# Reordering the opening of a conformer encoder step: tanh and the first modulation sums first, squares in one operation, the second modulation's sums between the first turns

## The chip, the cores and the metric

The kernel runs on one core of one Trainium2 chip. The metric is the device time of one execution in microseconds (us); the time before is the median of three runs. A core has five engines that run side by side and meet at semaphores: TensorE (PE, with its weight loads as PEld), VectorE (DVE), ScalarE (ACT), GpSimd (POOL) and SyncE (SP). Transfers are issued by SP and by ACT here; "SPq" and "ACTq" in the profile are those issues. Each engine takes its own instructions in the order in which the compiler has put them.

## The reference

One layer of a streaming encoder on 2048 prompt frames and 64 sample frames, D_MODEL = 1024, all in float32:

```python
mod = silu(c) @ w_ada + b_ada                 # 6 vectors of 1024 per batch
sh1, sc1, gt1, sh2, sc2, gt2 = split(mod, 6)
h = rms_norm(x, norm1_g) * (1 + sc1) + sh1
z = h @ w_in                                  # conv GLU pair | q | k | v | two gates
...                                           # conv branch, band attention, merge, output projection
x = x + gt1 * (merged @ w_o)
h2 = rms_norm(x, norm2_g) * (1 + sc2) + sh2
x = x + gt2 * ((silu(gate) * up) @ w_ffn_out) # gate, up = split(h2 @ w_ffn_in)
```

What matters here is the start: nothing of `z` can be multiplied before some of `sc1` and `sh1` (the product of silu(c) with `w_ada`) and the row norms of `x` are known.

## The kernel before

Float32 products are made from three products of a high and a low part (`mm3`): a weight `wst` is split into `whi` (a copy on ACT) and `wlo` (a subtraction on DVE or POOL), an activation `h` into `hh` and `hl` likewise. `Weights` (the object `W`) loads raw weights into at most three staging tiles `wst`, splits them in `split` and keeps up to `held` = 5 split ones; `W.reach` is how many `fill` may have split ahead, and `W.open("wst")` opens the second and third staging tile. `Slabs` (the object `M`) does the same for `w_ada`, in four buffers `wmod` of 512 KB; `M.get` and `M.done` use and free one, and a freed buffer is filled with the next slab.

The program is written in Python and unrolled. The compiler places the instructions on each engine: among those that it holds ready at a moment it takes the one written earliest, so an instruction written late can be placed early when its engine has a free moment. `with tc.issue_after(ins)` keeps every instruction of the block that runs on `ins`'s engine behind `ins`. The later blocks are interleaved by a planner in the program (`Stream`, `Lane`), which counts a load for each engine from assumed durations and lets side work step when these counts allow.

`first_block` computes the q columns of the first 576 rows, five row tiles `xs` (tile 0 is the sample's 64 rows, tiles 1 to 4 have 128 prompt rows), so that its parts can start as their inputs land:

- `setup` turns `c` into columns (`cc`), takes the tanh (`th`, ACT) for silu, and writes `cl` (DVE). `begun` holds the tanh and the write of `cl`. `vectors` transposes the loaded bias and norm vectors into `cols`.
- `modulation(ct)` multiplies `cl` with four slabs (`mod_sums`, into the PSUM tile `pa`: shift with two slabs, scale with two), copies the sums to `R` (`mod_rows`, DVE), and returns `rest`, which turns them into columns (`mod_columns`: four small products with `sel`, then DVE writes into `B1`, then again for `A1`). One call serves two of the eight 128-wide slices of D, `ct` and `ct + 1`.
- `scale_rows` takes the row norms: `square` (ACT, in two halves with a sum each, then a DVE add), `rsqrt_mean` (a small DVE operation `t`, a power on POOL `r`), and the scaling of the row tile on DVE.
- `turn(k)` transposes slice `k` of the five scaled row tiles into `pt` (PE), applies `A1` and `B1` (`h`, DVE), and splits it into `hh` (ACT) and `hl` (DVE).
- `product(i, k)` is the three matmuls of row tile `i` and slice `k` into `ps`. The loop over `k` runs `turn(k + 1)`, at even `k` the next `modulation(k + 2)`, and the five products. `product` needs split weight number `k // 2`.
- `first_rows` issues the loads of the five row tiles, `taps` (at `k == 2`) issues seven small loads on ACT, and `bias_rows`, written much later, loads the distance biases `rv` from ACT.

The order around the change before: the squares and scalings of tiles 0 and 1 are written ahead of `modulation(0)`, then `vectors`, `rest`, tiles 2 to 4, and `W.fill` (all behind `begun`); then `turn(0)`. In the loop, `modulation(2)` and `W.open("wst")` come at `k == 0` after the products of row tiles 0 and 1.

Of the kernel before, what the change touches and what calls it, by code (L numbers as in the profile page):

```python
# [8 lines left out]
F32 = mybir.dt.float32  # L9
F32R = mybir.dt.float32r  # L10
AF = mybir.ActivationFunctionType
# [5 lines left out]
P = 128  # L17
D = 1024
# [211 lines left out]
class Slabs:  # L230
# [8 lines left out]
    def fill(self):  # L239
        while len(self.ready) < min(len(self.keys), self.freed + self.held):  # L240
            (src,), a, b = self.source(self.keys[len(self.ready)])
            w = self.pool.tile([P, a, b], F32, tag="wmod", name="wmod", bufs=self.held)
            i = len(self.ready)
            (self.other if i < self.held and i % 2 else self.sync).dma_start(w, src)
            self.ready.append(w)

    def get(self, key):
# [364 lines left out]
def streaming_layer(ctx: ExitStack, tc: tile.TileContext, I, O):  # L612
    nc = tc.nc
# [121 lines left out]
    def rsqrt_mean(pool, ssq, n, width, count, bufs=5):  # L735
        t = pool.tile([P, 8], F32, tag="rs_t", bufs=bufs)
        r = pool.tile([P, 8], F32, tag="rs_r", bufs=bufs)
        dve.tensor_scalar(t[:n, :width], ssq, 1.0 / count, EPS, ALU.mult, ALU.add)
        stream.after("pool", "dve")
        gps.tensor_tensor(r[:n, :width], t[:n, :width], mhalf[:n, :width], ALU.pow)  # L740
        return r[:n, :width]
# [117 lines left out]
    def mod_rows(pa):  # L859
        R = temp("R", pa.shape)  # L860
        stream.after("dve", "pe")
        dve.tensor_copy(R, pa)
        return R

# [41 lines left out]

    def first_rows():
        places = ((wa, "x", 3), (wa, "x", 3), (wa, "x", 3), (wk, "kk", 1), (wk, "q2", 1))
        queues = (nc.sync, nc.sync, nc.scalar, nc.sync, nc.scalar)
        return [load_x(*tl, *place, q) for tl, place, q in zip(token_tiles(*PBLOCKS[0]), places, queues)]  # L910

    def first_block(xs):

        tiles = token_tiles(*PBLOCKS[0])
        vectors, taps, begun = setup()
        taps = taps()

        def scale_rows(a, b):
            for x_t, (t, n) in list(zip(xs, tiles))[a:b]:
                r = square(x_t, n)  # L920
                dve.tensor_scalar(x_t[:n], x_t[:n], r, None, ALU.mult)

        def modulation(ct):

            pa = ps_a.tile([P, 512], F32, tag="o", name="pa")
            cs = [slice(c6 * 2 * P, (c6 + 1) * 2 * P) for c6 in range(2)]

            with tc.issue_after(pe.last.ins):
                for c6, c in enumerate(cs):
                    mod_sums(pa[:, c], [("mod", c6, ct // 2, h, 0) for h in range(2)])  # L930
            R = mod_rows(pa)

            def rest():
                for c6, c in enumerate(cs):
                    mod_columns(pa[:, c], R[:, c], c6, ct, 1)

            return rest

        def turn(k):
            pt = ps_a.tile([P, 2, 512], F32, tag="s", name="pt")  # L940
            for i, (t, n) in enumerate(tiles):
                o = pt[:, 0, t : t + n] if i < 4 else pt[:, 1, :n]
                pe.transpose(o, xs[i][:n, k * P : (k + 1) * P], ident[:n, :n])
            h = wk.tile([P, QB + SMP], F32, tag="pr", name="h32", bufs=8)
            for a, e, o, w in ((0, SMP, pt[:, 0, :SMP], 1), (SMP, 448, pt[:, 0, SMP:448], 0), (448, 576, pt[:, 1, :P], 0)):
                dve.tensor_scalar(h[:, a:e], o, A1[:, k, w : w + 1], B1[:, k, w : w + 1], ALU.mult, ALU.add)

            for c in (slice(0, 448), slice(448, 576)) if not k else (slice(0, 576),):
                split(hh[:, k, c], hl[:, k, c], h[:, c])


        with tc.issue_after(begun[0]), tc.issue_after(begun[1]):
            scale_rows(0, 2)
            rest = modulation(0)
            vectors()
            rest()
            sums_turned = pe.last.ins
            with tc.issue_after(dve.last.ins):
                scale_rows(2, 5)
            with tc.issue_after(act.last.ins), tc.issue_after(dve.last.ins):  # L960
                W.reach = W.held
                W.fill()
        with tc.issue_after(sums_turned):
            turn(0)
        pss = [ps_g.tile([P, 512], F32, tag="gp", name="ps") for _ in tiles]
        ws = {}

        def product(i, k):
            t, n = tiles[i]
            if k // 2 not in ws:  # L970
                ws[k // 2] = W.get(("qkv", 0, k // 2))
            wh, wl = ws[k // 2]
            mm3(pss[i][:n], hh[:, k, t : t + n], hl[:, k, t : t + n], wh[:, k % 2], wl[:, k % 2], k == 0, k == KT - 1)
            if i == len(tiles) - 1 and k % 2:
                W.done()

        for k in range(KT - 2):
            if k == 2:
                with tc.issue_after(act.last.ins):
                    next(taps)  # L980
            turn(k + 1)
            if k and k % 2 == 0:
                rest = modulation(k + 2)
            for i in range(len(tiles)):
                if i == 2 and not k:
                    rest = modulation(k + 2)
                    W.open("wst")
                if i == (2 if k else 4) and k % 2 == 0:
                    rest()
                product(i, k)  # L990
        turn(KT - 1)
        for i, (t, n) in enumerate(tiles):
            for k in (KT - 2, KT - 1):
                product(i, k)
            work.start(qk_rows(pss[i], n, gqk[:, 0:1], q_d, t, None, i > 2))
        next(taps, None)

    bias = wk.tile([P, 640], F32, name="bias")

    def bias_rows():  # L1000
        rv = wk.tile([NH, 257], F32, tag="vv", name="rv", bufs=2)
        nc.scalar.dma_start(rv, I["rel_bias"].rearrange("l h r -> (l h) r"))
        rr = wk.tile([NH, 768], F32, tag="kk", name="rr", bufs=1)

        dve.tensor_scalar(rr[:, :256], rv[:, 1:], 8.0, None, ALU.mult)
        dve.memset(rr[:, 256:], 0.0)
        dve.tensor_scalar(rr[:, 256:], rr[:, 256:], rv[:, 256:], 8.0, ALU.add, ALU.mult)
        nc.scalar.dma_start(rb_d, rr)

        for r, c in ((0, 0), (HD, 576)):  # L1010
            dve.memset(bias[r : r + HD, c : c + HD], BIG)
# [122 lines left out]
        queue.dma_start(x_t[:n], rows(x_p, x_s, t, n))  # L1134
        return x_t

    def square(x_t, n):
        ssq = wk.tile([P, 2], F32, tag="ssq", name="ssq", bufs=3)
        for j in range(2):
            act.activation(temp("junk")[:n], x_t[:n, 512 * j : 512 * j + 512], AF.Square, accum_out=ssq[:n, j : j + 1])  # L1140
        stream.after("dve", "act")
        dve.tensor_tensor(ssq[:n, 0:1], ssq[:n, 0:1], ssq[:n, 1:2], ALU.add)
        return rsqrt_mean(wk, ssq[:n, 0:1], n, 1, D)
# [76 lines left out]
    YW = UW - HIST  # L1220
# [602 lines left out]
    for s, (lo, hi) in enumerate(CBLOCKS):  # L1823
# [195 lines left out]
        def rest(f, z, y):  # L2019


            if not seven(s, f):
                hidden(f, 1, y)
                return
            if "t" not in sums:
                sums["t"] = wk.tile([P, 4, 2, CW // 2], F32R, tag="m1", name="sums")
            at = lambda i: [sums["t"][:, i, l, :half] for l in range(2)]
            if f % 2 == 0:
                sums["a21"], sums["s3"] = (
                    wk.tile([P, CW // 2], F32, tag=name, name=name, bufs=1)[:, :half] for name in ("a21", "s3")  # L2030
                )
                stream.after("act", "dve")
                act.activation(sums["a21"], y, AF.Copy)
                stream.after("dve", "act")
                dve.tensor_tensor(y, z, sums["a21"], ALU.subtract)
                stream.after("act", "dve")
                split(*at(2), y)
                act.activation(sums["s3"], y, AF.Copy)
                return
            hidden(f, 1, y)  # L2040
            t = bank("gp")
            dve.tensor_tensor(t, y, sums["a21"], ALU.add)
            dve.tensor_tensor(y, y, sums["s3"], ALU.subtract)
# [253 lines left out]
```

## Time and profile before

| | |
|---|---|
| time, median of 3 runs (lowest to highest) | 2979.57 us (2976.84 to 2982.91) |
| the profiled execution's own time | 2979.5 us |
| its span, first to last instruction | 2977.7 us |
| TensorE busy | 2900.2 us (97% of the span) |
| VectorE busy | 2025.9 us (68%) |
| ScalarE busy | 1356.8 us (46%) |
| GpSimd busy | 1127.7 us (38%) |
| first matmul of the q product | starts 28.26 us into the span |
| mean granted TensorE clock | 0.995 |

The times in the profile count from the first instruction. A row of the timeline has the start, the duration, the engine (or its queue of issues), the line, the operation, what it writes and reads, shapes and a count, and in brackets how long the engine stood idle before it and what ended that. All engine calls pass through one helper, so nearly all rows carry its line, L102; tiles are told apart by their names. A row of the windows has the busy time of each engine in one stretch, the granted clock of TensorE, the busy share of the 16 DMA engines (which can come out slightly over 1) and the rate of transfers.

### The profile page before, as it was taken

How to read it: one execution, taken by the hardware profiler on the slowest of the kernel's cores; microseconds unless marked ns; L12 is line 12 of the kernel's file. 1: busy time of each engine (PE TensorE's matmuls, PEld its weight loads, DVE VectorE, ACT ScalarE, POOL GpSimd, SP SyncE). 2: the span in 40 equal slices, each digit the busy share in tenths (PEclk: the TensorE clock that was granted, in tenths of full speed). 3: DMA queues.
4: the chain of work that ended last, by engine and by line, in shares of the span. 5: the costliest groups of instructions: out<-in, count | busy, mean ns of one | idle time of the engine just before them, and what ended most of it. 6: DMA issues, size and time to landing. Idle time of an engine off the chain costs nothing.

```text
span 2977.7 us, 44838 instructions
## 1 busy us (share of the span) xinstructions
PE 2900.2 (97%) x16199; PEld 2593.1 (87%) x16199; DVE 2025.9 (68%) x3637; ACT 1356.8 (46%) x2441; POOL 1127.7 (38%) x727
## 2 busy tenths in 40 slices
PE   7999899999999999989999999999999999999999
PEld 4899777787888888888999999999999999999998
DVE  5797677767856886577777755666666557466666
ACT  2345642662456257464444345534444345344442
POOL 0201310111011102454466443255666741465667
PEclk9999999999999999999999999999999999999999
DMA  8889889878987798885444786333333975333333
GB/s 290 300 286 310 270 279 312 284 251 274 306 283 224 267 263 278 262 288 175 145 145 159 244 263 235 116 95 106 114 113 113 316 239 184 93 95 114 114 103 128
DMA packets 467723, 628.05 MB, mean 211 GB/s; under 512 B 36276, under 2 KB 314664, under 8 KB 467501
## 3 DMA queue, kind: packets, MB, share of 16 engines
q1 hardware_dynamic: 453456, 605.58, 62.8%
q10 hardware_dynamic: 14045, 19.60, 1.9%
q8 instruction: 127, 2.08, 0.3%
q14 instruction: 95, 0.78, 0.1%
HBM read 476.53 MB, written 148.54 MB: 210 GB/s over the span
## 4 chain that ended last, share of the span: by engine, by line
PE 82%; DVE 7%; DMA 4%; ACT 2%; issue 2%; POOL 2%; SPq 0%; ACTq 0%; POOLq 0%; DVEq 0%
PE ps L102 53%; PE pd L102 16%; PE pw L102 6%; DVE y L102 2%; PE sc L102 2%; PE po L102 2%; PE ptp L102 2%; DVE wlo L102 1%; PE pt L102 1%; DMA kk<-k_d 1%; ACT whi L102 1%; PE pa L102 1%; POOL r L102 1%; DVE pw L102 1%; DMA wst<-in_w_in 0%
## 5 line engine op out<-in xcount | busy, mean ns | idle before, releaser
L102 PE MATMUL ps<-t,whi 128*128 128x384 f32 (+1 forms) x2112 | 503.1, 322 | 8.7 <-ACT t L102 4.9
L102 POOL TENSOR_TENSOR wlo<-wst,whi 128x1024 fp32r<-128x1024 f32 (+1 forms) x156 | 356.4, 2294 | 279.0 <-ACT whi L102 262.6
L102 ACT ACTIVATE whi<-wst 128x1024 fp32r<-128x1024 f32 (+1 forms) x263 | 256.8, 979 | 331.2 <-PE ps L102 119.8
L102 PE MATMUL ps<-b,whi 128*128 128x384 f32 (+1 forms) x1584 | 381.7, 326 | 7.0 <-DVE early L102 3.6
L102 PEld LDWEIGHTS ps<-t,whi 128*128 128x128 f32 x2112 | 367.8, 188 | 16.3 <-ACT t L102 5.1
L102 DVE SCALAR_TENSOR_TENSOR y<-u,wd,y 128x512 f32<-128x512 f32 (+1 forms) x480 | 369.0, 773 | 6.3
L102 PE MATMUL ps<-hh,whi 128*128 128x512 f32 (+2 forms) x992 | 361.7, 365 | 0.0
L102 DVE TENSOR_TENSOR acc<-acc,pd 128x512 f32<-128x512 f32 x464 | 311.7, 685 | 62.7 <-PE pd L102 60.2
L102 PE MATMUL ps<-hl,whi 128*128 128x512 f32 (+2 forms) x992 | 345.6, 348 | 0.0
L102 PE MATMUL ps<-hh,wlo 128*128 128x512 f32 (+2 forms) x992 | 345.4, 348 | 0.0
L102 PE MATMUL ps<-t,wlo 128*128 128x384 f32 (+1 forms) x1056 | 339.4, 322 | 0.8 <-POOL wlo L102 0.7
L102 PE MATMUL pd<-whi,hid 128*128 128x512 f32 x972 | 314.8, 390 | 0.0
L102 PEld LDWEIGHTS ps<-b,whi 128*128 128x128 f32 x1584 | 278.7, 189 | 13.1 <-DVE early L102 4.5
L102 POOL TENSOR_TENSOR r<-t,mhalf 128x1 f32<-128x1 f32 (+3 forms) x68 | 83.6, 1232 | 462.1 <-DVE t L102 457.0
L102 PE MATMUL ps<-b,wlo 128*128 128x384 f32 (+1 forms) x792 | 257.3, 325 | 0.0
L102 ACT ACTIVATE pr<-pr,sm 128x640 f32<-128x640 f32 (+3 forms) x272 | 200.1, 747 | 112.1 <-DVE sm L102 109.5
L102 PEld LDWEIGHTS pd<-whi,hid 128*128 128x128 f32 x972 | 182.5, 188 | 37.7 <-ACT hid L102 0.7
L102 PEld LDWEIGHTS ps<-hh,wlo 128*128 128x128 f32 x992 | 186.7, 188 | 21.6
L102 PEld LDWEIGHTS ps<-hh,whi 128*128 128x128 f32 x992 | 187.2, 189 | 18.5 <-issue 1.6
L102 PEld LDWEIGHTS ps<-hl,whi 128*128 128x128 f32 x992 | 187.5, 189 | 15.5 <-issue 1.4
L102 PEld LDWEIGHTS ps<-t,wlo 128*128 128x128 f32 x1056 | 198.2, 188 | 2.2 <-POOL wlo L102 1.3
L102 PE MATMUL pd<-wlo,hid 128*128 128x512 f32 x508 | 198.6, 391 | 0.0
(226 smaller groups left out, 6170.6 us busy)
## 6 DMA issues: line engine op xcount, KB each, us to landing
whi<-w_din_h SPq DMA_DIRECT2D x72, 512.0 KB, 6.5
wlo<-w_din_l SPq DMA_DIRECT2D x72, 512.0 KB, 8.4
wst<-sum_d SPq DMA_DIRECT2D x132, 256.0 KB, 2.7
wfo<-in_w_ffn_out SPq DMA_DIRECT2D x64, 512.0 KB, 3.2
wmod<-in_w_ada SPq DMA_DIRECT2D x46, 512.0 KB, 6.5
sum_d<-ws SPq DMA_DIRECT2D x88, 256.0 KB, 2.8
wst<-in_w_ffn_in SPq DMA_DIRECT2D x84, 256.0 KB, 3.1
wst<-in_w_in SPq DMA_DIRECT2D x40, 512.0 KB, 8.8
```

The costliest lines, as they stand in the source:

```text
L102: self.last = f(*args, **kw)
```

## The change

- `setup`, tanh and `cl` stay; the load of row tile 4 goes from ACT's queue to SP's, and the load of `rv` is kept behind the last square.
- `modulation(0)` is written first, ahead of any row. `R` is kept behind the last DVE instruction written before it. `vectors` follows behind the sums and `R`, then the rows of tiles 2 and 0, then `rest`, then tiles 1, 3 and 4.
- A square takes one ACT operation over 1024 columns with one sum, written to a junk tile in the place of `y`, in place of two operations of 512 and a DVE add.
- `W.reach` is 1 at first, so one weight is split behind the last square and scaling; the next ones are split after `turn(1)`.
- `modulation(2)` moves from the loop to ahead of it, with `turn(0)` written between its two halves; the second half stands behind `turn(0)` on PE and its `R` behind `turn(0)` on DVE. `W.open("wst")` follows it, its loads kept behind the last slab's load.

```diff
@@ Slabs.fill
-            (self.other if i < self.held and i % 2 else self.sync).dma_start(w, src)
+            self.last = (self.other if i < self.held and i % 2 else self.sync).dma_start(w, src)
@@ first_rows
-        queues = (nc.sync, nc.sync, nc.scalar, nc.sync, nc.scalar)
+        queues = (nc.sync, nc.sync, nc.scalar, nc.sync, nc.sync)
@@ first_block
-        def scale_rows(a, b):
-            for x_t, (t, n) in list(zip(xs, tiles))[a:b]:
-                r = square(x_t, n)
+        junk = wk.tile([P, 4, YW], F32, tag="y", name="junk").rearrange("p a b -> p (a b)")[:, :D]
+
+        def scale_rows(*order):
+            for i in order:
+                x_t, (t, n) = xs[i], tiles[i]
+                r = square(x_t, n, junk)
                 dve.tensor_scalar(x_t[:n], x_t[:n], r, None, ALU.mult)
-        def modulation(ct):
+        def modulation(ct, between=None):
...
-            with tc.issue_after(pe.last.ins):
-                for c6, c in enumerate(cs):
+            for c6, c in enumerate(cs):
+                with tc.issue_after(pe.last.ins):
                     mod_sums(pa[:, c], [("mod", c6, ct // 2, h, 0) for h in range(2)])
-            R = mod_rows(pa)
+                    if between and not c6:
+                        between()
+            with tc.issue_after(dve.last.ins):
+                R = mod_rows(pa)
...
         with tc.issue_after(begun[0]), tc.issue_after(begun[1]):
-            scale_rows(0, 2)
             rest = modulation(0)
-            vectors()
-            rest()
-            sums_turned = pe.last.ins
-            with tc.issue_after(dve.last.ins):
-                scale_rows(2, 5)
+            with tc.issue_after(pe.last.ins), tc.issue_after(dve.last.ins):
+                vectors()
+                scale_rows(2, 0)
+                rest()
+                scale_rows(1, 3, 4)
+                begun_rows.append(act.last.ins)
             with tc.issue_after(act.last.ins), tc.issue_after(dve.last.ins):
-                W.reach = W.held
+                W.reach = 1
                 W.fill()
-        with tc.issue_after(sums_turned):
-            turn(0)
+        rest = modulation(2, lambda: turn(0))
+        with tc.issue_after(M.last.ins):
+            W.open("wst")
@@ loop over k
             turn(k + 1)
+            if not k:
+                with tc.issue_after(act.last.ins), tc.issue_after(dve.last.ins):
+                    W.reach = W.held
+                    W.fill()
             if k and k % 2 == 0:
                 rest = modulation(k + 2)
             for i in range(len(tiles)):
-                if i == 2 and not k:
-                    rest = modulation(k + 2)
-                    W.open("wst")
@@ bias_rows
-        nc.scalar.dma_start(rv, I["rel_bias"].rearrange("l h r -> (l h) r"))
+        with tc.issue_after(begun_rows[0]):
+            nc.scalar.dma_start(rv, I["rel_bias"].rearrange("l h r -> (l h) r"))
@@ square
-    def square(x_t, n):
+    def square(x_t, n, junk=None):
         ssq = wk.tile([P, 2], F32, tag="ssq", name="ssq", bufs=3)
+        if junk is not None:
+            act.activation(junk[:n], x_t[:n], AF.Square, accum_out=ssq[:n, 0:1])
+            return rsqrt_mean(wk, ssq[:n, 0:1], n, 1, D)
```

More of the change, by code (lines that the diff above doesn't have):

```diff
@@ L998, in streaming_layer @@
     bias = wk.tile([P, 640], F32, name="bias")
+    begun_rows = []
     def bias_rows():
         rv = wk.tile([NH, 257], F32, tag="vv", name="rv", bufs=2)
-        nc.scalar.dma_start(rv, I["rel_bias"].rearrange("l h r -> (l h) r"))
+        with tc.issue_after(begun_rows[0]):
+            nc.scalar.dma_start(rv, I["rel_bias"].rearrange("l h r -> (l h) r"))
         rr = wk.tile([NH, 768], F32, tag="kk", name="rr", bufs=1)
```

## The prediction

> **What bounds the kernel now.** I read the page's head first: TensorE is busy for nearly the whole span.
>
> ```profile
> span 2977.7 us, 44838 instructions
> PE 2900.2 (97%) x16199; PEld 2593.1 (87%) x16199; DVE 2025.9 (68%) x3637; ACT 1356.8 (46%) x2441; POOL 1127.7 (38%) x727
> ```
>
> PE's idle time is 2977.7 - 2900.2 = 77.5 us. The change touches only the opening, so the second view is the windows of 5 us there.
>
> ```profile
> 5.00:10.00 5.00, 0.00 (x0) 0.00 (x0) 0.13 (x1) 0.00 (x0) 0.00 (x0) 1.00 1.08 345
> 10.00:15.00 5.00, 2.58 (x25) 1.25 (x29) 1.57 (x10) 3.95 (x10) 1.06 (x4) 1.00 1.00 349
> 15.00:20.00 5.00, 3.65 (x24) 2.17 (x16) 2.05 (x6) 3.29 (x11) 0.56 (x1) 1.00 1.05 359
> 20.00:25.00 5.00, 2.02 (x7) 0.88 (x5) 3.35 (x12) 1.43 (x3) 1.93 (x3) 1.00 1.07 369
> 25.00:30.00 5.00, 3.09 (x10) 2.21 (x11) 4.26 (x10) 2.74 (x5) 0.00 (x0) 1.00 0.40 118
> 30.00:35.00 5.00, 5.00 (x42) 2.72 (x42) 4.28 (x5) 1.56 (x2) 0.00 (x0) 1.00 0.32 93
> ```
>
> Two things stand here. From 5 to 25 us the transfers are full (share 1.00 to 1.08, 345 to 369 GB/s) and no compute engine is; from 25 to 35 us the transfers fall to 0.40 and 0.32. So the compute is late with its first steps, and the transfers then stand still because no buffer comes free. The timeline shows who is late.
>
> ```profile
> 2.71 0.60 ACTq L1134 DMA_DIRECT2D x_t<-in_x_prompt  x1
> 4.95 0.17 DVE L102 COPY cc<-pt 128x16 f32<-128x16 f32 x1 [3.00 <-PE pt L102]
> 9.04 0.30 ACTq L1002 DMA_DIRECT2D rv<-in_rel_bias  x1
> 10.42 0.35 ACTq L1134 DMA_DIRECT2D x_t<-in_x_prompt  x1
> 10.80 1.28 ACT L102 ACT_TABLE_LOAD   x1 [10.80 <-DMA x_t<-in_x_prompt]
> 12.10 0.22 ACT L102 ACTIVATE th<-cc 128x16 f32<-128x16 f32 x1
> 12.79 3.64 PE L102 MATMUL pa<-wmod,cl 128*32 128x256 f32 x32 [1.17 <-DVE cl L102]
> 13.44 0.61 ACT L102 ACTIVATE junk<-x_t 128x512 f32<-128x512 f32 x1
> 13.93 2.93 SPq L244 DMA_DIRECT2D wmod<-in_w_ada  x4
> 16.50 0.69 DVE L102 COPY R<-pa 128x512 f32<-128x512 f32 x1 [1.18 <-PE pa L102]
> 16.70 0.63 ACT L102 ACTIVATE junk<-x_t 128x512 f32<-128x512 f32 x1 [1.95 <-PE pa L102]
> 16.91 9.41 SPq L375 DMA_DIRECT2D wst<-in_w_in  x3
> 20.30 0.19 ACT L102 ACTIVATION_READ_ACCUMULATOR junk<-x_t 128x1 f32 x1
> 20.39 1.04 ACT L102 ACTIVATE whi<-wst 128x1024 fp32r<-128x1024 f32 x1
> 23.22 0.16 DVE L102 TENSOR_SCALAR t<-ssq 128x1 f32<-128x1 f32 x1
> 24.04 0.75 DVE L102 TENSOR_SCALAR x_t<-x_t,r 128x1024 f32<-128x1024 f32 x1 [0.66 <-POOL r L102]
> 24.70 1.22 DVE L102 TENSOR_TENSOR wlo<-wst,whi 128x1024 fp32r<-128x1024 f32 x1
> 27.23 1.38 PE L102 MATMUL pt<-ident,x_t 64*128 64x64 f32 x5 [1.91 <-DVE h L102]
> 28.26 0.77 PE L102 MATMUL ps<-whi,hh 128*64 128x512 f32 x1
> 31.10 2.38 PE L102 MATMUL pa<-wmod,cl 128*32 128x256 f32 x32
> 32.24 2.73 SPq L244 DMA_DIRECT2D wmod<-in_w_ada  x4
> 33.41 0.51 PE L102 MATMUL ps<-whi,hh 128*128 128x512 f32 x1
> ```
>
> ACT issues `rv` at 9.04 and row tile 4 at 10.42, each after waiting, and in its order the table load and the tanh stand behind them. The tanh's input `cc` was there at 4.95 + 0.17 = 5.12. The chain names that wait: a row transfer from 2.71 to 10.41.
>
> ```profile
> 2.71 7.70 DMA x_t<-in_x_prompt
> ```
>
> **The change, step by step.** The sum is made on the profiled execution: 2979.5 us, of which 2977.7 are span and 1.8 lie around it; it stands 0.07 us under the median of 2979.57.
>
> *Tanh and first sums.* With both issues gone from ACT ahead of it, ACT is free at 2.71 + 0.60, the table load ends near 4.6, and the tanh runs at 5.15. From tanh to first sum it took 12.79 - 12.10 = 0.69, so the sums can begin at 5.84. They then wait for slabs: all four were issued before the row tile that landed at 10.41, and a slab of 0.52 MB at 345 GB/s takes 1.5 us, so I put the last slab at 8.9 (latest 10.4). A slab's sums are 3.64 / 4 = 0.91, so they end at 9.8 to 11.3; I take 10.0, by the order of issue. `R` ends at 10.7 and not at 17.19. The bias columns are no longer hidden under the tanh's wait, but cost DVE under 1 us in a window where it is 1.57 of 5 us busy.
>
> *Row norms.* Tile 4's load moves past SP's other issues: behind tile 3, ahead of the first `wst`, which lands at most one 0.52 MB transfer (1.5 us) later; `rv` has 8 KB and is read far later. Behind 10.41 come 0.26 MB for tile 0 and three times 0.52 MB, 1.83 MB at 349 to 359 GB/s or 5.2 us, plus small vectors: tile 4 lands at about 16. One square is one operation of 1024 columns; the nearest row, a copy of 1024, takes 1.04, plus 0.19 to read the sum, against 2 x 0.61 and an add: about even on ACT (bounds -0.2 to +0.2 each), one DVE instruction fewer. ACT keeps pace with the landings, and the wait of 1.95 at the third tile's square, whose scratch tile was tied to PE, has no cause left. So tile 4's square ends near 17.4. From `t` to the scaled tile it took 24.79 - 23.22 = 1.57, POOL's power in it: tile 4 is scaled at 19.1 instead of 24.79. POOL gets the same five powers, two of them in another order, and nothing else waits in it. `whi` follows on ACT (17.4 to 18.5), `wlo` behind the scaling (to 20.3 instead of 25.92).
>
> *First turn.* From the scaled tile to the first product it was 28.26 - 24.79 = 3.47, which gives 22.6 as the earliest start, if nothing else stands on PE.
>
> *Second modulation's sums.* They do stand there. Their slabs could be issued from about 10 us instead of 13.93, but the transfers are full, so their landing hardly moves. I take the measured landing:
>
> ```profile
> DMA to landing us min/median/max: 5.6/5.6/5.6
> DMA to landing us min/median/max: 6.5/6.5/6.5
> ```
>
> The first row is of the four slabs issued from 13.93, the second of the four from 32.24. The last of the first four is issued by 16.86 and lands at 22.1 to 23.4; its sums (0.91 slow) end at about 23.9. `turn(1)` follows with 1.38, and the first product starts at 25.3, not 28.26. PE's order binds it now: turn 0 and products queue behind the slabs, which is what is late next. But PE no longer has the 2.38 of sums to do between products. Before, six product matmuls ran from 28.26 to 31.10 and the sums to 33.41; after, six from 25.3 at the same slow pace end at 28.1. The same state is reached 5.3 us earlier; at the fast pace (next part) 6.7. I take 6.0. `R` of that modulation now stands on DVE behind `hl` of turn 0; queued behind it are turn 1's `h` and the `wlo` of weights 1 and 2, all needed after 28, so it costs nothing unless the slabs are late. If the cover goes (DVE late by more than 3 us) it costs what is above that.
>
> *Weights and slabs after that.* The third `wst` of the SP row at 16.91 waited for the first one's `wlo` until 25.95; it goes at about 20.5. The third modulation's slabs are released by the second's sums, from about 20 instead of 32.24. These five transfers are 2.6 MB, 7.3 us at 359 GB/s, and fill the hole of 25 to 35 us: they land by about 33.5, where the last slab of 32.24 landed near 34.9 + 6.5 = 41.4. PE reaches the third sums at 41.64 - 6.0 = 35.6, so no new wait.
>
> ```profile
> 41.64 1.93 PE L102 MATMUL pa<-wmod,cl 128*32 128x256 f32 x32
> 58.38 0.64 PE L102 MATMUL pa<-wmod,cl 128*32 128x256 f32 x8 [1.83 <-DMA wmod<-in_w_ada]
> 59.98 0.63 PE L102 MATMUL ps<-whi,hh 128*128 128x512 f32 x1
> 60.41 0.63 PE L102 MATMUL ps<-wlo,hh 128*128 128x512 f32 x1
> 63.34 0.40 PE L102 MATMUL ps<-wlo,hh 128*128 128x512 f32 x1
> ```
>
> *The fourth modulation's wait.* Before, PE stood 1.83 us for the last slab of this part and then ran nine matmuls with a start every 0.43 us (60.41 - 59.98) behind it. In the wide rows the time of one falls from 0.63 to 0.40, so I count 0.2 x 9 = 1.8 for them. Together 3.6 us. After the change the transfers are ahead by the filled hole (10 us at 0.36 mean share, 6.4 us gained), and the weights that stood between these slabs are loaded earlier. Bounds: all 3.6 saved, or, if the slab lands only 4 us earlier while PE comes 6 earlier, 2 us lost. I take 1.5 saved, the nearer to the measured hole.
>
> Sum: 6.0 + 1.5 = 7.5 us. 2979.5 - 7.5 = **2972.0**.
>
> *A rule weighed against it.* The rows say that a product matmul takes 0.63 after idle PE and 0.40 in a run, with the granted clock in the profile at 1.00 in 25 to 35 us. The Trainium skill (TensorE: Matmul & The Clock Gate, Part 1: The HAM clock gate) states that the array runs at half rate by default and is released only after a window of about 3.4 us of sustained work. This case's trace agrees in size: 0.43 us between starts at first, later about half. By that rule it is open whether the waits for slabs between 18 and 24 us leave the array slow at the first product; that is the difference between 5.3 and 6.7 above, and where it stays slow for long it is the rival below.
>
> **The rivals.**
>
> *Opening gained, later lost (2977).* The stretch behind is nearly full on other resources:
>
> ```profile
> 100.00:150.00 50.00, 49.33 (x268) 41.09 (x267) 41.76 (x63) 19.44 (x30) 11.87 (x6) 1.00 0.94 318
> 150.00:200.00 50.00, 47.94 (x305) 43.73 (x305) 48.11 (x76) 18.23 (x32) 3.73 (x6) 1.00 0.84 301
> ```
>
> DVE is at 48.11 of 50 and the transfers at 0.94. If these and not PE set that stretch, PE comes early and waits there: two thirds are given back, 2979.5 - 2.5 = 2977. Against it: PE itself is at 49.33 and 47.94, and DVE's work there waits for PE's output, so it moves along; the transfers have won 6.4 us of their own.
>
> *The order does not do what it says (2979).* If the compiler sets some other ready issue on ACT ahead of the tanh, or slabs 5 and 6 of `w_ada` hold turn 0 to 24, the start stays near 28 and what is left is the moved sums, under 2.4, eaten by slow matmuls. Against: the `issue_after` on `rv`, and the load taken from ACT.
>
> *Slow array (slower, 2987).* Thinly fed from 25 us on, PE stays at the slow pace. Each matmul then costs 0.2 more; there are 60 for `k` = 0 to 3, plus transposes and sums of 7 us that about double: 12 to 15 us, so 2979.5 - 6.0 + 13.5 = 2987. It decides at about 30 slow matmuls (6.0 / 0.2). For it: the waits for slabs in the middle of PE's work. Against it: before, PE went fast within some 4 us of the first product despite the same feed (0.51 at 33.41, after 0.77 at 28.26).
>
> **How the numbers follow.** The forecast has 0.60, in which what is won reaches the end; given back later 0.20; no effect 0.08; slow array 0.12. What a measurement of this kernel can tell from no change is about 0.2%, 6 us. The forecast's own range is 2966 to 2976 (savings from 5.3 - 2 = 3.3 to 6.7 + 3.6 = 10.3, and up to 3 more if PE is fast from its first product); about 0.15 of its chance lies above 2973.6, where it counts as the same. Faster: 0.60 x 0.85 = 0.51, and 0.02 of the second case, which may give back less: 0.53. Slower, above 2985.5, is the slow array's 0.12. The same is what is left, 0.35. The range is 2964 to 2985: outside it lie most of the slow array's case and the far end of the forecast.
>
> **What would show it.** Right: tanh near 5.2 and first sums from 5.8, `R` near 10.7; tile 4 scaled near 19; second sums ending near 24 with PE waiting for `wmod` before; first product near 25; transfers in 25 to 35 us above 0.8; no wait for `wmod` at the fourth sums. Wrong: a tanh still behind an issue on ACT; a first product at 28 or later; matmuls of 0.63 beyond 32 us; the opening ahead by 6 us at 77 us but not at 300.

## The result and the profile after

The changed kernel takes 2969.75 us (median of 10 runs, 2964.79 to 2974.64), beside 2979.31 us (10 runs) for the kernel before: a ratio of 0.9969 with a 95% interval of 0.9960 to 0.9979, or 9.2 us (6.3 to 11.9). The forecast of 2972.0 was 2.3 us too high. The profiled execution took 2969.84 us. On its page PE is as busy as before (2900.2) in a span that is 9.6 us shorter:

```profile
span 2968.1 us, 44826 instructions
PE 2900.5 (98%) x16199; PEld 2593.4 (87%) x16199; DVE 2024.0 (68%) x3632; ACT 1357.8 (46%) x2431; POOL 1129.0 (38%) x727
```

So the change took idle time of PE away and nothing else. The same windows of the opening as in the prediction (busy us of PE, PEld, DVE, ACT and POOL; granted clock, share of the transfers, GB/s):

```profile
5.00:10.00 5.00, 0.05 (x1) 0.00 (x0) 0.17 (x1) 1.50 (x2) 0.00 (x0) 1.00 0.86 274
10.00:15.00 5.00, 4.06 (x34) 1.66 (x34) 1.19 (x5) 1.96 (x3) 0.00 (x0) 1.00 0.99 294
15.00:20.00 5.00, 2.71 (x9) 1.93 (x9) 3.53 (x16) 4.81 (x9) 3.76 (x8) 1.00 1.05 382
20.00:25.00 5.00, 4.34 (x28) 1.22 (x28) 3.33 (x6) 0.10 (x2) 0.46 (x1) 1.00 1.09 356
25.00:30.00 5.00, 4.99 (x20) 3.27 (x21) 3.44 (x8) 1.96 (x4) 0.00 (x0) 1.00 1.08 362
30.00:35.00 5.00, 5.00 (x28) 3.94 (x28) 3.18 (x8) 1.33 (x2) 0.00 (x0) 1.00 1.00 328
```

The hole in the transfers between 25 and 35 us (0.40 and 0.32 before) is filled: 1.08 and 1.00. A new, smaller one stands at 5 to 10 us: 0.86, where before had 1.08. The timeline tells how the steps came out:

```profile
8.09 0.35 ACTq L1144 DMA_DIRECT2D x_t<-in_x_prompt  x1
8.47 1.28 ACT L102 ACT_TABLE_LOAD   x1 [8.47 <-DMA r<-in_norm_g]
9.76 0.21 ACT L102 ACTIVATE th<-cc 128x16 f32<-128x16 f32 x1
10.45 3.64 PE L102 MATMUL pa<-wmod,cl 128*32 128x256 f32 x32 [5.40 <-DVE cl L102]
12.09 4.96 SPq L244 DMA_DIRECT2D wmod<-in_w_ada  x4
14.16 0.69 DVE L102 COPY R<-pa 128x512 f32<-128x512 f32 x1 [3.77 <-PE pa L102]
19.09 1.37 POOL L102 TENSOR_TENSOR r<-t,mhalf 128x1 f32<-128x1 f32 x2 [1.00 <-DVE t L102]
19.67 1.58 DVE L102 TENSOR_SCALAR x_t<-x_t,r 128x1024 f32<-128x1024 f32 x2 [0.60 <-POOL r L102]
20.60 1.08 PE L102 MATMUL pa<-wmod,cl 128*32 128x256 f32 x8 [2.14 <-DMA wmod<-in_w_ada]
21.16 1.22 DVE L102 TENSOR_TENSOR wlo<-wst,whi 128x1024 fp32r<-128x1024 f32 x1
23.87 2.22 PE L102 MATMUL pa<-wmod,cl 128*32 128x256 f32 x16
27.08 0.77 PE L102 MATMUL ps<-whi,hh 128*64 128x512 f32 x1
29.79 0.49 PE L102 MATMUL ps<-whi,hh 128*128 128x512 f32 x1
37.95 1.93 PE L102 MATMUL pa<-wmod,cl 128*32 128x256 f32 x32
49.96 0.83 PE L102 MATMUL pt<-ident,x_t 64*128 64x64 f32 x5 [1.36 <-DVE h L102]
50.72 2.15 PE L102 MATMUL pa<-wmod,cl 128*32 128x256 f32 x32
```

The tanh comes at 9.76, not at 5.15: ACT still has the load of row tile 2 ahead of it. ACT's issue before that one ended at 2.67, and this one ran only at 8.09; the profile puts the end of the wait down to the landing of a small vector load. The first product comes at 27.08 instead of 28.26, only 1.2 us earlier, but by then the second sums are done. The waits for slabs at the fourth modulation (1.83 before) are gone; in their place PE waits 1.36 for `h`.

To see where the time is won I count PE's matmuls, in order of start, and compare the start of the one with the same number. This is "the lead" below (us):

```
number   before   after: start   lead
   120    39.17          35.48    3.7
   200    52.58          47.30    5.3
   240    58.63          52.48    6.2
   280    67.64          59.91    7.7
   320    76.44          68.71    7.7
   600   124.38         116.64    7.7
  2000   335.55         332.03    3.5
  6000  1100.34        1089.86   10.5
 16198  2971.96        2962.35    9.6
```

Behind the opening the lead is 7.7 us; later it goes down to 3.5 and up again. In the two traces PE's matmuls come in another order up to number 636 (near 129 us before) and in the same order from there on, so what moves the lead later is waits and the clock. The granted clock shows it. Of the kernel before:

```profile
59.40:62.80 3.40, 3.40 (x11) 2.56 (x9) 0.38 (x1) 0.00 (x0) 0.00 (x0) 0.50 1.03 414
62.80:66.20 3.40, 3.40 (x21) 2.52 (x21) 0.70 (x4) 0.00 (x0) 0.00 (x0) 1.00 1.05 407
```

In 3.4 us at a clock of 0.50 PE starts 11 matmuls, in the next 3.4 us at 1.00 it starts 21. That stretch at half rate follows the wait of 1.83 at 58.38. Of the kernel after, the same place:

```profile
45.00:60.00 15.00, 13.63 (x94) 9.69 (x93) 8.20 (x20) 2.88 (x4) 0.00 (x0) 1.00 1.06 389
```

No half rate here. So 1.6 us of the lead come from this one stretch of this one profile of before: the lead grows from 6.2 at number 240 to 7.7 at number 280 as before passes it. Every lead at number 320 below is taken against the same profile and holds these 1.6 us. From 40 us to the last matmul the records of both profiles hold 27.3 us at half rate, in stretches of 3.4 or 6.8 us, but at other places: before at 59, 350, 421, 909, 1199 and twice near 1320 us, after at 180, 262, 347, 996 and twice near 1310. Each costs up to 1.7 us. The Trainium skill (TensorE: Matmul & The Clock Gate, Part 1) says that the gate is decided in windows of about 3.4 us and that idle windows bring the half rate back. The stretches here agree in length; but of the 3.4 us ahead of the one at 59.4 PE was idle for 1.8, not for all.

### The profile page after: what moved, and what is told of

The parts are those of the page before. It is cut to its first block, busy times and chain, and to the rows that moved or that the text cites. A ratio compares the mean times of both kernels' runs of the same rounds, so it can differ in the third digit from the quotient of the medians.

```text
span 2968.1 us, 44826 instructions
## 1 busy us (share of the span) xinstructions
PE 2900.5 (98%) x16199; PEld 2593.4 (87%) x16199; DVE 2024.0 (68%) x3632; ACT 1357.8 (46%) x2431; POOL 1129.0 (38%) x727
## 4 chain that ended last, share of the span: by engine, by line
PE 83%; DVE 7%; DMA 4%; ACT 2%; POOL 2%; issue 2%; SPq 0%; ACTq 0%; DVEq 0%; POOLq 0%
PE ps L102 54%; PE pd L102 16%; PE pw L102 6%; DVE y L102 2%; PE po L102 2%; PE sc L102 2%; PE ptp L102 2%; DVE wlo L102 1%; PE pt L102 1%; PE pa L102 1%; ACT whi L102 1%; DMA tg<-g_d 1%; POOL r L102 1%; DVE pw L102 1%; POOL wlo L102 0%
## 5 line engine op out<-in xcount | busy, mean ns | idle before, releaser
L102 POOL TENSOR_TENSOR r<-t,mhalf 128x1 f32<-128x1 f32 (+2 forms) x68 | 84.3, 1242 | 448.1 <-DVE t L102 436.9
```

The source lines that it names most:

```text
L102: self.last = f(*args, **kw)
```

## The experiments

All are timed beside runs of the kernel before on the same chip. "Time" is the difference of the medians; the ratio, with its 95% interval, is not the quotient of these medians, so the two columns can differ by up to 1.6 us. "Squares only", "without reach 1" and "rows ahead of vectors" were timed on the chip of the changed kernel's second timing; the others are compared with it only through the kernel before. In the last two rows the lead is counted without the extra matmuls.

| kernel | tanh | first product | lead, number 320 | time | ratio |
|---|---|---|---|---|---|
| changed kernel | 9.76 | 27.08 | 7.7 | -9.6 | 0.9969 (0.9960 to 0.9979) |
| the same again | 8.21 | 25.83 | 9.8 | -9.5 | 0.9971 (0.9961 to 0.9981) |
| loads only | 8.34 | 27.29 | 3.7 | +0.2 | 1.0002 (0.9994 to 1.0011) |
| squares only | 12.14 | 26.35 | 1.3 | -0.8 | 1.0001 (0.9992 to 1.0010) |
| without the squares | 9.05 | 27.53 | 4.4 | -2.8 | 0.9996 (0.9987 to 1.0005) |
| the same again | 8.52 | 26.56 | 4.4 | -7.7 | 0.9973 (0.9963 to 0.9984) |
| without the second modulation's move | 8.20 | 22.91 | 10.4 | -2.5 | 0.9995 (0.9986 to 1.0004) |
| the same again | 8.17 | 23.27 | 8.9 | -5.1 | 0.9980 (0.9971 to 0.9989) |
| without reach 1 | 8.70 | 26.63 | 8.3 | -5.7 | 0.9986 (0.9976 to 0.9996) |
| all rows from SP | 5.21 | 28.73 | 3.5 | +2.3 | 1.0009 (1.0000 to 1.0017) |
| rows ahead of vectors | 5.26 | 29.58 | 3.5 | +3.2 | 1.0009 (1.0001 to 1.0018) |
| PE kept busy | 8.53 | 25.04 | 8.9 | -11.8 | 0.9959 (0.9946 to 0.9971) |
| the same again | 8.78 | 25.23 | 8.1 | -9.1 | 0.9970 (0.9958 to 0.9982) |

Theory: the change wins what the prediction listed, each part its share. Rivals: one part does it all; what is won in the opening does not reach the end; the tanh itself is what counts.

### The changed kernel again

No edit.

> The changed kernel once more, beside the parts of it and on their chip. Theory (the parts do not add up, the whole is what counts): again 0.31% faster than before, 9 to 10 us, and the lead at the 320th matmul again 7 to 8.5 us. Rival (the first comparison was a favourable one, as the parts came to 0 to 3 us): 3 to 6 us faster.

Measured: 0.9971, and the lead at number 320 was 9.8, more than the 7 to 8.5 expected. The size of the result stands, and the lead reaches the end: from 7.7 and 9.8 us at number 320 it came to 9.6 and 13.0 at the last matmul of the two executions, beside 9 us in the medians. Between executions the opening itself differs: the load of row tile 2 was issued at 6.53 here and at 8.09 in the other, and tanh, slabs and first product with it. Here the products also ran at the fast pace from the first one on (25.83), and the seventh started at 27.29, not at 29.79.

### One part alone

Loads only, on the kernel before (`begun_rows[0]` is the last square):

```diff
-        queues = (nc.sync, nc.sync, nc.scalar, nc.sync, nc.scalar)
+        queues = (nc.sync, nc.sync, nc.scalar, nc.sync, nc.sync)
...
-        nc.scalar.dma_start(rv, I["rel_bias"].rearrange("l h r -> (l h) r"))
+        with tc.issue_after(begun_rows[0]):
+            nc.scalar.dma_start(rv, I["rel_bias"].rearrange("l h r -> (l h) r"))
```

> The kernel before with one part of the change: row tile 4 is loaded from SP and the load of the biases stands behind the last square. Theory (the parts of the opening add up, and the tanh is one of them): the tanh runs near 9.8 us as in the changed kernel (12.10 before), the first product comes 1 to 2 us earlier than 28.26, and the time is 2977 to 2978 against 2979.3 of before. Rival (the rows on VectorE set the start, the tanh does not): first product within 0.5 us of 28.26 and no change of the time.

Measured: the tanh at 8.34, and yet the first sums only at 12.32, because PE had the transpose of the bias vectors in its order ahead of them and waited for their landing. No change of the time (+0.2, ratio 1.0002), though its profile shows a lead of 3.7 at 77 us. So the tanh came 3.8 us earlier and the sums only 0.5 us (12.79 before): what an earlier tanh is worth was not tested here, because the order of `vectors` ahead of the sums took it away.

Squares only, on the kernel before:

```diff
-                r = square(x_t, n)
+                r = square(x_t, n, junk)
```

> The kernel before with the squares in one operation and nothing else. Theory (the rows on ACT and VectorE bound the start of before after the tanh, and its third square waited 1.95 us for its scratch tile): tile 4 is scaled 1 to 2 us earlier, first product at 26.5 to 27.5, and the time 1 to 2 us less. Rival (about even on ACT, as the prediction said): no change within 1 us.

Measured: first product 1.9 us earlier (26.35, as the theory had it), lead 1.3, time -0.8 and a ratio whose interval holds 1. PE's wait for the slabs of the fourth modulation grew from 1.83 to 2.5 us.

### All but one part

Without the squares: the changed kernel with `square(x_t, n)` in two halves.

```diff
-                r = square(x_t, n, junk)
+                r = square(x_t, n)
```

> The changed kernel with the squares in two halves as before. The opening should be the same within 0.5 us at the 320th matmul (7.7 us ahead of before), by either theory. The planner's counts are then those of before, and its order of all later work too. Theory (the later order is worth the difference of the two traces behind 77 us, 9.6 - 7.7 = 1.9 us): time 2971.7. Rival (what is won in the opening reaches the end whatever the later order): 2969.8 within 1 us. Third: the order of before gives part of it back: over 2973.

> The changed kernel with the squares in two halves, a second time. Theory (ACT is on the path of the rows in the changed kernel, so the longer squares delay tile 4, the split of the first weight and the third slabs): the lead at the 320th matmul is again near 4 us, and the time 5 to 8 us over the changed kernel. Rival (execution to execution scatter): lead near 7 us, time within 3 us of the changed kernel.

Measured: a lead of 4.4 us in both profiles and not 7.7 to 9.8, so in these four profiles the squares are worth 3 to 5 us of the lead at number 320 once the rest is done. The theory about the planner's counts falls: its loss was to come behind 77 us, and this one is there by then. The time was 2.8 us under before on one chip (with a ratio whose interval holds 1) and 7.7 on the other. So of the second run's theory the lead came, and not the 5 to 8 us over the changed kernel; there its rival had the size. DVE's order differs in the opening. In the first of these runs (DVE's rows of the last three tiles):

```profile
18.96 0.14 DVE L102 TENSOR_TENSOR ssq<-ssq 128x1 f32<-128x1 f32 x1
19.96 0.75 DVE L102 TENSOR_SCALAR x_t<-x_t,r 128x1024 f32<-128x1024 f32 x1 [0.67 <-POOL r L102]
20.62 0.15 DVE L102 TENSOR_TENSOR ssq<-ssq 128x1 f32<-128x1 f32 x1
21.63 0.76 DVE L102 TENSOR_SCALAR x_t<-x_t,r 128x1024 f32<-128x1024 f32 x1 [0.66 <-POOL r L102]
22.30 0.15 DVE L102 TENSOR_TENSOR ssq<-ssq 128x1 f32<-128x1 f32 x1
23.30 0.75 DVE L102 TENSOR_SCALAR x_t<-x_t,r 128x1024 f32<-128x1024 f32 x1 [0.66 <-POOL r L102]
```

Each row goes through add, `t`, POOL and scaling before DVE takes up the next: 1.67 us a row (22.30 - 20.62), although ACT had the last square's sum at 19.32. In the changed kernel DVE does `t` for two rows, POOL takes both powers (19.09, x2), and both scalings follow (19.67, 1.58): tile 4 is scaled at 21.25 and not at 24.05. It is not the add as such that forces this: the kernel before has the same adds, and there DVE took two rows together.

```profile
20.53 0.22 DVE L102 TENSOR_TENSOR ssq<-ssq 128x1 f32<-128x1 f32 x2
20.71 0.22 DVE L102 TENSOR_SCALAR t<-ssq 128x1 f32<-128x1 f32 x2
21.54 1.58 DVE L102 TENSOR_SCALAR x_t<-x_t,r 128x1024 f32<-128x1024 f32 x2 [0.60 <-POOL r L102]
```

Nor is this where the lead is lost. The first products start 0.5 and 0.7 us later than in the changed kernel's two profiles, and at number 120 the leads are 4.2 and 5.5, beside 3.7 and 6.3. The loss stands behind that: PE waits for `hh`, in the first of these runs

```profile
43.57 0.24 ACTq L833 DMA_DIRECT2D r<-in_w_dw  x1
43.86 1.06 ACT L102 ACTIVATE whi<-wst 128x1024 fp32r<-128x1024 f32 x1 [6.02 <-DMA wmod<-in_w_ada]
44.82 0.67 ACT L102 ACTIVATE hh<-h 128x576 fp32r<-128x576 f32 x1
45.54 0.69 PE L102 MATMUL ps<-whi,hh 128*64 128x512 f32 x1 [1.77 <-ACT hh L102]
```

and in the second

```profile
52.05 1.06 ACT L102 ACTIVATE whi<-wst 128x1024 fp32r<-128x1024 f32 x1 [8.48 <-DMA wst<-in_w_in]
53.01 0.67 ACT L102 ACTIVATE hh<-h 128x576 fp32r<-128x576 f32 x1
53.73 0.45 PE L102 MATMUL ps<-whi,hh 128*64 128x512 f32 x1 [2.08 <-ACT hh L102]
```

In both, `hh` stands in ACT's order behind a `whi` that comes late: in the first behind an issue that waited (ACT's issue before it had ended at 40.13), in the second for its weight to land. A stretch at half rate begins with the end of the one wait (45.5) and 1.9 us behind the other (55.6). The changed kernel's profiles have neither the wait nor the stretch there. Why the weights come later here, and whether the row-by-row order is behind it, stays open.

Without the move of the second modulation: turn 0 ahead of the loop, the sums at `k == 0` behind two row tiles' products.

```diff
-        rest = modulation(2, lambda: turn(0))
-        with tc.issue_after(M.last.ins):
-            W.open("wst")
+        with tc.issue_after(pe.last.ins):
+            turn(0)
...
+                if i == 2 and not k:
+                    rest = modulation(k + 2)
+                    with tc.issue_after(M.last.ins):
+                        W.open("wst")
```

> The changed kernel with the second modulation put back into the loop, behind the products of row tiles 0 and 1 at k = 0, turn 0 ahead of it. Theory (the move is worth PE's 2.4 us of sums between the products): the first product starts earlier than 27.08, near 24 to 25, but the sums stand again between the products and the opening at the 320th matmul is 1 to 3 us behind the changed kernel; time 2971 to 2973. Rival (PE waits for the slabs' landing in either place): the state after six products and the sums is the same within 0.5 us and the time is 2969.8.

> The changed kernel with the second modulation in the loop, a second time: its first profile had a lead of 10.35 us at the 320th matmul and its median was only 1 to 3 us under before. Theory (that profile was of a favourable execution: its time was 3.7 us under its own median): the lead of this one is 5 to 8 us and the time again 1 to 3 us under before. Rival (the lead is there each time and is lost behind the opening, where TensorE falls back to half rate): lead again near 10 us at the 320th matmul, time again 1 to 3 us under before, and more half-rate stretches behind 60 us than in the changed kernel.

Measured: the first product at 22.91 and 23.27, 2.6 to 4.2 us earlier than in the changed kernel, and leads of 10.4 and 8.9, no smaller than the changed kernel's. So PE's 2.4 us of sums were not what the move saved: up to number 320 the move is worth nothing. But the time is only 2.5 and 5.1 us under before, and in both profiles the lead shrinks up to number 2000 (near 335 us before), 10.4 to 4.9 and 8.9 to 3.6; in the changed kernel it went from 7.7 to 3.5 in one and only from 9.8 to 8.7 in the other.

The rival of the second of these runs asked for more half-rate stretches than in the changed kernel; there were not more (20.5 us behind 40 us in both of its profiles, 27.3 and 20.5 in the changed kernel's). From number 320 to number 2000, before and in this variant's two profiles:

```profile
76.44:335.55 259.11, 252.46 (x1681) 231.21 (x1680) 210.60 (x388) 128.30 (x264) 51.05 (x45) 1.00 0.87 291
66.09:330.63 264.54, 254.73 (x1681) 232.56 (x1680) 210.51 (x388) 127.84 (x264) 50.25 (x45) 0.99 0.85 286
67.52:332.00 264.48, 255.68 (x1681) 234.01 (x1680) 210.25 (x388) 128.29 (x264) 50.30 (x45) 0.99 0.86 287
```

Of the 5.4 us lost here, PE stands idle for 3.2 and 2.2 us more than before, and its matmuls take 2.3 and 3.2 us longer, with 3.4 and 6.8 us at half rate. In the changed kernel's profiles the idle time grows by 1.0 and 0.8.

One thing goes with it: in this variant 24 of PE's matmuls between number 956 and number 1799 stand in another place than before, in the changed kernel none behind number 636. The variants below with the rows from SP, the rows ahead of the vectors and PE kept busy have the same other order there, and the one without reach 1 a similar one. All seven profiles with another order lose 3.4 to 7.4 us of lead in this stretch; the six that have the order of before from number 704 on lose at most 4.2, and four of them at most 1.1. So leaving out a part also changes the order of later work, and the times of these variants hold both. That the order is the cause was not tested. Why this variant keeps less of its lead thus stays open. Both profiled executions of it were about 3 us faster than its median, so the profile does not show the usual case.

Without reach 1: `W.reach` at 5 from the start.

```diff
-                W.reach = 1
+                W.reach = W.held
```

> The changed kernel with W.reach at 5 from the start, so that the splits of the second and third weight may stand ahead of turn 1. Theory (the splits are not what the products wait for): lead at the 320th matmul and time as the changed kernel within 1.5 us. Rival (the splits on ACT and VectorE come ahead of turn 1's h and delay the products): 1 to 3 us slower than the changed kernel.

Measured: the same lead (8.3), and -5.7 instead of -9.5 on the same chip: 3.8 us, a little more than the rival's 1 to 3 (the two intervals of the ratio overlap), but not at the rival's place, since the opening shows no delay. The lead falls to 4.9 at number 2000, where this variant has its other order.

### An earlier tanh

All rows from SP:

```diff
-        queues = (nc.sync, nc.sync, nc.scalar, nc.sync, nc.sync)
+        queues = (nc.sync,) * 5
```

> The changed kernel with the load of row tile 2 also issued by SP, so that no row load stands on ACT ahead of the tanh. The tanh should run at about 5.3 us instead of 9.76 and the first sums begin at about 6. Theory (transfers and the landing of the slabs set PE's start): the first product moves by at most 1 us from 27.08 and the time by at most 1 us from 2969.8. Rival (the tanh still sets the start, as the prediction had it): first product at 25.3 or earlier, time 2967 to 2968.

Rows ahead of vectors:

```diff
-    next(vectors_)
     xs = first_rows()
+    next(vectors_)
```

> The changed kernel with the six small vector loads issued behind the five row loads instead of ahead of them. Theory (in the opening the queues wait for transfers that are still under way, ACT at the load of row tile 2 until 8.09, so the transfers fall to 0.86 between 5 and 10 us): tanh at 5.2, transfers above 1.0 from 5 us on, second sums and first product 1 to 2 us earlier than 26.09 and 27.08, time 1 to 2 us below the changed kernel. Rival (the vectors are now late, and the columns of the first modulation with them): A1 later than 18.9 by 2 us or more and no gain.

Both put the tanh where the prediction wanted it, at 5.2, and both are about 12 us slower than the changed kernel and if anything 0.1% slower than before. The timeline of the first (the square of row tile 2, the split of the first weight, the first product):

```profile
5.90 1.08 PE L102 MATMUL pa<-wmod,cl 128*32 128x256 f32 x8 [0.93 <-DVE cl L102]
15.31 1.06 ACT L102 ACTIVATE junk<-x_t 128x1024 f32<-128x1024 f32 x1 [9.89 <-DMA x_t<-in_x_prompt]
21.09 1.04 ACT L102 ACTIVATE whi<-wst 128x1024 fp32r<-128x1024 f32 x1
28.73 0.78 PE L102 MATMUL ps<-whi,hh 128*64 128x512 f32 x1
```

The first sums begin at 5.90, but the first square in ACT's order now waits until 15.31 (11.62 in the changed kernel) for a tile whose load is now the third of five on SP and no longer the first of all; all squares, the split (21.09, not 18.98) and the product are later. In the second, the rows share the transfers with the slabs. PE's waits for slabs from 10 to 80 us (sum, count, longest, us):

```profile
PE pa L102 <- DMA wmod<-in_w_ada: 6.8, 4, 3.6
```

and one of its windows:

```profile
15.00:20.00 5.00, 2.23 (x13) 1.11 (x5) 1.64 (x6) 3.97 (x7) 1.89 (x6) 1.00 0.46 129
```

The last of the first four slabs is there only at 14.64, SP issues the next four from 16.83 (12.09 in the changed kernel), and the transfers fall to 0.46 between 15 and 20 us. So with the tanh 4.5 us earlier the rows came late in the one kernel and the slabs in the other, and the first product went from 27.08 to 28.73 and 29.58. That does not tell what the tanh alone is worth: no run has it early with rows and slabs in time. Part of their time is lost later: in both profiles a lead of 3.5 at number 320 has become -2.1 at the last matmul, and 7.4 us of it go in the stretch up to number 2000 described above.

### PE kept busy

Ten matmuls of 128x128 into a tile that nobody reads, six ahead of the first sums, four ahead of the second (the code's `...` leaves out the lines between):

```diff
+        def keep_busy(times):
+            warm = ps_g.tile([P, 512], F32, tag="gp", name="warm")
+            with tc.issue_after(pe.last.ins):
+                for _ in range(times):
+                    pe.last = nc.tensor.matmul(warm[:, :P], ident, sel, start=True, stop=True)
+
+        keep_busy(6)
...
+        keep_busy(4)
         rest = modulation(2, lambda: turn(0))
```

> The changed kernel with ten 128x128 matmuls on TensorE that compute nothing of the result, six ahead of the first sums and four ahead of the second. Theory (TensorE's half rate in the opening is a cost of its own, 0.43 us between product starts instead of 0.23, and work ahead of the products ends it): the granted clock comes back to 1.0 before the first product, the products start at the fast pace, lead at the 320th matmul 1 to 2.5 us over the changed kernel's 7.7 to 9.8, time 1 to 2.5 us below it. Rival (the fast pace only waits longer for the slabs): first product moved by under 0.5 us and no gain.

> The changed kernel with the ten extra matmuls, a second time, since its first comparison had few runs. Theory (the extra work is worth about 2 us over the changed kernel): 10 to 13 us faster than before. Rival (the first comparison was favourable, as it could be with an interval of 2.5 us to each side): 8 to 10 us, the changed kernel's own value.

Measured: the first product at 25.04 and 25.23, but it still ran at the slow pace (0.78), so the mechanism is not the one expected. The ten matmuls stand in the trace as twenty instructions:

```profile
4.81 2.93 PE L922 MATMUL warm<-sel,ident 128*128 128x128 f32 x12
15.17 1.06 PE L922 MATMUL warm<-sel,ident 128*128 128x128 f32 x8
```

Counted without them, the leads at number 320 are 8.9 and 8.1, within the changed kernel's 7.7 and 9.8. The time is -11.8 (5 runs) and -9.1. Against the changed kernel's -9.6 and -9.5 that is no difference that can be told: the rival came, the extra work is worth nothing that shows.

## Why the prediction was right or wrong

The sum was right in size: 7.5 us forecast, a lead of 7.7 and 9.8 us behind the opening in two executions, 9.2 us in the time. That is in part luck. Its first term, 6.0, came to 3.7 us in the first execution and 6.3 in the second (the lead at number 120); its second, 1.5, came to 4.0 and 3.5 (what the lead gains from there to number 280), of which 1.6 are the half-rate stretch of the one profile of before. In the first execution two misses cancel each other; in the second the first term is right and the second too small. What was in the terms:

- *Tanh and first sums*: wrong. The step "ACT is free at 2.71 + 0.60" failed: the load of row tile 2 was itself an issue that waits for a landing, and it moved from 2.71 to 8.09. The chain of before had shown such a wait one issue later, and I took it to vanish with that issue. The sums began at 10.45 and not at 5.84, `R` ended at 14.85 and not at 10.7. The two kernels with the tanh at 5.2 won nothing by it, but their rows or slabs came later, so what this step would have been worth alone is not shown.
- *Row norms*: a size. Tile 4 was scaled at 21.25, forecast 19.1; the slabs and rows came about 1.5 us later than I had them, with the transfers at 0.86 in 5 to 10 us. "About even on ACT" held for the length of a square, 1.06 beside 2 x 0.61, and the term was set at nothing. Without the squares the lead at number 320 is 3 to 5 us smaller, but the 2.8 us at tile 4 are not the reason: the first product is only 0.5 to 0.7 us later, and the rest is lost behind number 120, in waits for `hh` of 1.8 and 2.1 us and in the clock.
- *Second modulation's sums*: the mechanism came (PE waited 2.14 us for a slab at 20.60, the sums ended at 26.09, forecast 23.9; the first product at 27.08, forecast 25.3). After six products, before stood at 33.41 and after at 29.79: 3.6 us, forecast 5.3 to 6.7; in the second execution, at the fast pace from the first product, after stood there at 27.29, which is 6.1 us and inside the forecast. That this move is a gain in the opening fell: without it the lead at number 320 was as large. The time without it was 4 to 7 us worse, lost behind number 320, for which the prediction had no term.
- *Weights and slabs after that*: right. The hole in the transfers was filled, and the third sums at 37.95 had no wait.
- *The fourth modulation's wait*: right in kind, too small. Forecast 1.5 of 3.6 us; the wait and the half-rate stretch both went, against a new wait of 1.36 for `h`, and the lead grew from 3.7 at number 120 to 7.7 at number 280. In the second execution a wait of 0.6 for these slabs was left.
- *Later lost*: the rival did not come about for the changed kernel's median, but leads were lost behind the opening in other kernels: in their profiles 3.7 at number 320 became 0.1 at the last matmul (loads only), 3.5 became -2.1 (all rows from SP) and 10.4 became 7.5 (without the second modulation's move). Whether by the resources that the rival named is not shown.
- *Slow array*: did not come; the products were at the fast pace from 29.79, in the second execution from 25.83. In the kernel before I read a granted clock of 1.00 for 25 to 35 us beside a start every 0.43 us; the clock column cannot be right there, since the kernel's first record of the clock is at 32.1 us. The 1.00 in the opening's rows of after is no better: the first record there is at 30.0. In the second profile of the changed kernel the records begin earlier and show the half rate in the opening:

```profile
15.20:25.40 10.20, 6.45 (x41) 1.93 (x39) 7.14 (x16) 4.57 (x9) 2.73 (x4) 0.50 1.07 366
25.40:60.00 34.60, 32.62 (x211) 23.56 (x211) 21.99 (x43) 10.29 (x13) 0.00 (x0) 1.00 1.04 344
```

Not tested alone is the largest part of the change: the first modulation's sums and `vectors` ahead of the rows were in every kernel whose lead at number 320 is 4.4 or more, and no run leaves them out of the whole. That they carry the gain follows only from the other parts not carrying it alone.

## What to carry to other kernels

When an issue waits in front of an instruction on the critical chain, ask what the next issue in that queue will wait for, and what the waiting holds back: here the two kernels with an early tanh won nothing, because with it the row loads came late or ahead of the slabs. Follow a delay to the engine that counts before you give it a price: tile 4 was scaled 2.8 us later without the squares, and the first product came only 0.5 to 0.7 us later. Judge a part by leaving it out of the whole as well as by doing it alone, and look whether leaving it out has changed the order of later work. And when you compare instructions by their number, count the ones that you added.

## What the runs showed of the hardware that was not expected

TensorE drops to half rate for stretches of 3.4 us or multiples of it in the middle of a kernel that is 98% busy: six to eight such windows behind 40 us in nearly every profile here, 17.1 to 27.3 us in all. In all fourteen profiles PE stood idle for at least 1.4 of the 3.4 us ahead of each of these stretches; but not every such gap is followed by one (in the first profile of the changed kernel, idle times of 1.9 us at 299 and 2.4 us at 414 are not). Where they fall differs between two executions of the same kernel (at 180, 262 and 347 us in one, at 343 us alone in the other, over the first 400 us), and with up to 1.7 us each they are as large as the steps in which the lead changed. Even one variant, without the squares, came out at 0.9996 on one chip and 0.9973 on another beside the same kernel before, more than the intervals say.
